# Attention heads in pairs, both token halves transposed in one slot, and another piece left unshifted

## The chip, the cores and the metric

The kernel runs on one core of a Trainium2 chip. The metric is the device time of one execution in microseconds, the median of the runs shown; lower is better.

## What is computed

One layer of a hybrid decoder trunk, 256 tokens by 2048 channels, all float32:

```
h    = rms_norm(x, gain)
proj = einsum('bsd,de->bse', h, w_in)      # 2048 x 8192: h_conv b c z_conv q k v z_attn, 1024 columns each
conv = b * causal_conv_width3(c * h_conv);  y_conv = rms_norm(conv) * silu(z_conv)
q, k = rms_norm per head (8 heads x 128)
s    = q k^T * 128**-0.5, masked to k_pos <= q_pos      # SEQ is one block, so plain causal attention
attn = softmax(s) v;                        y_attn = rms_norm(attn) * silu(z_attn)
out  = x + concat(y_conv, y_attn) @ w_out   # 2048 x 2048
```

## The kernel before

**Products.** Every large product is made from parts: an operand is split into a high half (`wh`, `xs[..., 0]`, `yh`, type fp32r) and the rest (`wl`, `xs[..., 1]`, `yl`), and three products replace one (`by_parts`, L111 to L113; for the channel-major units two instructions, L489 with 512 moving columns for both halves of x and L490 with 256). An fp32r product is one record in the trace. A few small products have plain f32 operands instead, here called *whole*: the q and k transposes (L229, four of 128x128 a call), the first quarter of a head's scores (L258), the transposes of the probabilities (L289, three a head) and the second half of the values' product (L305). A whole product that is no transpose is two records.

**Pieces.** The weights come in 160 pieces of 512 KB, each read by a DMA into `raw` (three buffers), split by ScalarE into `wh` (L481) and by VectorE into `wl` (L482; five buffers each), and used by TensorE. 48 pieces are of kind A (q, k, v for two column halves c: q0 k0 v0 q1 k1 v1, eight pieces each, accumulated token-major in `acc`), then 80 of kind B (20 units of four pieces: the gate `a` of attention, units 0 to 3, then h, c, b, z), then 32 of kind Y (the output product; the last four pieces accumulate in `aux`). They are named A0 to A47, B0 to B79, Y0 to Y31 below; the loop index is j, so B0 is j = 48.

**Order.** The order on each engine is the order of the program text. In iteration j the loop issues the load of piece j+6, the split of piece j+3 and the matmuls of piece j, and then runs what `at(slot, f, ...)` has put under slot j. So all small work stands behind the matmuls of its piece on TensorE, and behind the split of piece j+3 on ScalarE and VectorE. `finish_a` places the work of attention, by the index e of the unit's last piece: for q and k the squares (e+1), norm (e+4, e+5; for q0 later, since it waits for the norm of x), transposes of token half t at e+6+t and their evacuation a slot later (`then`); for v the four heads of the half, head i from slot b = e+2+2i: scores, mask, exponent, normalize, p_transposes, p_transposed, attend, attended at b to b+7. So slots b+4 and b+6 of one head are also slots of the next ones.

**Island.** A run of TensorE instructions between the matmuls of two pieces that holds whole products is called an island here.

**PSUM.** `aux` has four buffers of one bank, used in turn by scores, transposes and values' products; `acc` has two of two banks.

**The shift.** `wh` lies 16 elements further into its buffer in every piece of kind B (`shift`, L465), except in the one piece named by `UNSHIFTED`, a pair (unit, first k-tile):

```
SHIFT, UNSHIFTED = 16, (3, KT // 2)
shift = SHIFT if kind == "B" and (n, k) != UNSHIFTED else 0
```

(3, 8) is B14. Pieces of kind A and Y are not shifted.

Of the kernel before, what the change touches and what calls it, by code (L numbers as in the profile page):

```python
# [17 lines left out]
P = 128  # L18
SEQ = 256
NT = SEQ // P  # L20
DM = 2048
KT = DM // P
DG = 1024
CW = 512
HD = 128
NH = DG // HD
HPC = CW // HD
# [16 lines left out]
SINGLE = 4  # L44
NWARM = 10

SHIFT, UNSHIFTED = 16, (3, KT // 2)


@with_exitstack  # L50
def hybrid_layer(ctx: ExitStack, tc: tile.TileContext, xT, x, w_a, w_b, w_out, par, out):
    nc = tc.nc
# [11 lines left out]
    def aux():  # L64
        return ps.tile([P, CW], F32, name="aux", bufs=4)
# [12 lines left out]
    a = aux()  # L78
    for i in range(NWARM):
        nc.tensor.matmul(a.rearrange("p (a b) -> p a b", b=P), warm, warm[:, None, :].to_broadcast([P, CW // P, P]),  # L80
                         start=i == 0, stop=i == NWARM - 1)
# [18 lines left out]
    def at(slot, f, *args):  # L100
        todo.setdefault(slot, []).append((f, args))
# [6 lines left out]
    def by_parts(acc, stationary, moving, first, last):  # L108

        (sh, sl), (mh, ml) = stationary, moving  # L110
        nc.tensor.matmul(acc, sh, mh, start=first, stop=False)  # L111
        nc.tensor.matmul(acc, sh, ml, start=False, stop=False)  # L112
        nc.tensor.matmul(acc, sl, mh, start=False, stop=last)  # L113
# [83 lines left out]
    qk_0, v_sb, sq, ssq_h, r_h, qn = {}, {}, {}, {}, {}, {}  # L197
# [34 lines left out]
    def k_parts(c):  # L232
        return (y[:, c * HPC:(c + 1) * HPC] for y in (yh, yl))

    def q1_parts(c):
        n = HPC * P // SEQ
        return (y[:, KT // 2 + c * n:KT // 2 + (c + 1) * n].rearrange("p a (b t) -> p (a b) t", t=P) for y in (yh, yl))
# [14 lines left out]

    sc, mx, pr, pT, den = {}, {}, {}, {}, {}

    def scores(h):
        c, i = divmod(h, HPC)
        a = sc[h] = aux()
        nc.tensor.matmul(a[:, :P], qk_0["q", c][:, i], qk_0["k", c][:, i], start=True, stop=True)  # L258
        by_parts(a[:, P:3 * P], [q[:, i] for q in q1_parts(c)], [k[:, i] for k in k_parts(c)], True, True)

    parts = ((0, slice(0, P)), (1, slice(P, 3 * P)))

# [35 lines left out]

    def attend(h):
        c, i = divmod(h, HPC)  # L300
        a = sc[h] = aux()
        vh, vl, v1 = (v[:, i * HD:(i + 1) * HD] for v in v_sb[c])
        hi, lo, p1 = pT[h]
        by_parts(a[:, :SEQ], (vh, vl), (hi, lo), True, False)
        nc.tensor.matmul(a[:, P:SEQ], v1, p1, start=False, stop=True)  # L305

    def attended(h):
        nc.scalar.activation(oT[:, h], sc[h][:, :SEQ], AF.Copy)
# [85 lines left out]
    def finish_a(name, c, acc, e):  # L394
        key, col = (name, c), G_Q if name == "q" else G_K
        late = X_RMS if (name, c) == A_ORDER[0] else 0
        for t in range(NT):
            if name == "v":
                at(e + 1, v_done, c, t, acc[:, t])
            else:  # L400
                at(e + 1, head_squares, key, t, acc[:, t])
                at(max(e + 4 + t, late + 2 ), head_norm, key, t, acc[:, t])
                at(max(e + 6, late + 4) + t, then, max(e + 7, late + 5) + t, head_transposes, head_transposed, key, t, col)
        if name != "v":
            at(e + 2, head_sums, key)
            at(max(e + 2, late + 1), head_rms, key)
            return
        for i in range(HPC):
            h, b = c * HPC + i, e + 2 + 2 * i
            for d, f in enumerate((scores, mask, exponent, normalize, p_transposes, p_transposed, attend, attended)):  # L410
                at(b + d, f, h)

    def finish_b(name, g, acc, e):
        if name == "a":
            at(e + 1, z_done, g, acc)
            at(e + 2, z_silu, g)
            at(A_DONE + 2 * g, lambda: z_gate(g, oT[:, g * GPT:(g + 1) * GPT], KT // 2, G_A))
        elif name == "h":
            at(e + 1, h_done, g, acc)
            at(e + 2, h_scaled, g)  # L420
        elif name == "c":
            at(e + 1, c_done, g, acc)
            at(e + 2, conv, g)
        elif name == "b":
            at(e + 1, b_done, g, acc)
            at(e + 2, lambda: add_squares("c", yc[g]))
        else:
            at(e + 1, z_done, g, acc)
            at(e + 2, z_silu, g)
            at(e + 3, lambda: z_gate(g, yc[g], 0, G_C))  # L430
# [89 lines left out]
    e = ends["B", len(B_ORDER) - 2]  # L520
# [9 lines left out]
    for j, (kind, n, _, k, last, pk, _) in enumerate(pieces):  # L530
# [10 lines left out]
        elif kind == "A":  # L541
            for i in range(pk):
                if j < SINGLE:

                    for n, (s, m) in enumerate(((0, 0), (0, 1), (1, 0))):
                        for t in range(NT):
                            nc.tensor.matmul(acc[:, t], xs[:, k + i, s, t * P:(t + 1) * P], w[m][:, i],
                                             start=k + i == 0 and n == 0, stop=False)
# [5 lines left out]
            if last:  # L554
                finish_a(*A_ORDER[n], acc, j)
# [65 lines left out]
```

## Time and profile before

| | |
|---|---|
| median of 3 runs | 466.1 us (466.03 to 466.13) |
| the profiled execution | 466.41 us, its span 464.6 us, so 1.8 us around it |
| TensorE busy | 458.4 us, 99% of the span |
| VectorE, ScalarE busy | 304.3 us (66%), 241.4 us (52%) |
| weight loads on TensorE (PEld) | 392.0 us (84%) |
| HBM read | 88.11 MB, 194 GB/s over the span |

How to read it: PE is TensorE's matmuls, PEld its weight loads, which overlap them; DVE is VectorE, ACT ScalarE, SP SyncE, which issues the loads. The ends of matmuls are modelled, so they overlap in the rows and busy time says little: the distance from one *start* to the next is what a matmul takes of TensorE's time. A row of a timeline gives start, duration, engine, line, what is written and read, and the count of equal instructions merged.

### The profile page before, as it was taken

How to read it: one execution, taken by the hardware profiler on the slowest of the kernel's cores; microseconds unless marked ns; L12 is line 12 of the kernel's file. 1: busy time of each engine (PE TensorE's matmuls, PEld its weight loads, DVE VectorE, ACT ScalarE, POOL GpSimd, SP SyncE). 2: the span in 40 equal slices, each digit the busy share in tenths (PEclk: the TensorE clock that was granted, in tenths of full speed). 3: DMA queues.
4: the chain of work that ended last, by engine and by line, in shares of the span. 5: the costliest groups of instructions: out<-in, count | busy, mean ns of one | idle time of the engine just before them, and what ended most of it. 6: DMA issues, size and time to landing. Idle time of an engine off the chain costs nothing.

```text
span 464.6 us, 6426 instructions
## 1 busy us (share of the span) xinstructions
PE 458.4 (99%) x2418; PEld 392.0 (84%) x2418; DVE 304.3 (66%) x441; ACT 241.4 (52%) x336; POOL 17.3 (4%) x23
## 2 busy tenths in 40 slices
PE   8999999999999999999999999999999999999996
PEld 5888788888888898888888888888888888888885
DVE  4996866657485657678767676666667775555541
ACT  5965646564535677655645554454545453433320
POOL 1000100002020000000000000000000110001000
PEclk9999999999999999999999999999999999999999
DMA  8977764746565645556666556656666668776731
GB/s 278 299 212 230 231 206 137 223 136 181 141 209 170 200 141 157 172 186 189 213 198 190 192 183 196 204 188 195 193 196 190 190 217 271 231 235 209 247 121 47
DMA packets 27151, 90.63 MB, mean 195 GB/s; under 512 B 3184, under 2 KB 3696, under 8 KB 27120
## 3 DMA queue, kind: packets, MB, share of 16 engines
q1 hardware_dynamic: 26496, 88.51, 60.9%
q0 software_dynamic: 480, 1.57, 1.0%
q8 instruction: 19, 0.31, 0.3%
q10 hardware_dynamic: 144, 0.13, 0.1%
q14 instruction: 12, 0.10, 0.1%
HBM read 88.11 MB, written 2.10 MB: 194 GB/s over the span
## 4 chain that ended last, share of the span: by engine, by line
PE 88%; DMA 4%; DVE 3%; ACT 2%; issue 1%; POOL 0%; SPq 0%; ACTq 0%; DVEq 0%
PE acc L489 31%; PE acc L490 16%; PE acc L111 12%; PE acc L113 12%; PE acc L112 12%; DMA raw<-in_w_a_dram 4%; ACT wh L481 1%; PE aux L111 1%; PE aux L112 1%; PE aux L113 1%; DVE wl L482 1%; PE aux L229 1%; PE aux L289 1%; ACT xs L174 0%; DVE sums_x L130 0%
## 5 line engine op out<-in xcount | busy, mean ns | idle before, releaser
L482 DVE TENSOR_TENSOR wl<-raw,wh 128x1024 fp32r<-128x1024 f32 x156 | 190.5, 1224 | 97.7 <-ACT wh L481 96.8
L481 ACT ACTIVATE wh<-raw 128x1024 fp32r<-128x1024 f32 x156 | 165.0, 1059 | 112.2 <-PE acc L113 53.0
L489 PE MATMUL acc<-xs,wh 128*128 128x512 f32 x640 | 218.6, 390 | 0.0
L490 PE MATMUL acc<-xs,wl 128*128 128x256 f32 x640 | 176.8, 276 | 0.0
L489 PEld LDWEIGHTS acc<-xs,wh 128*128 128x128 f32 x640 | 120.2, 188 | 24.9
L490 PEld LDWEIGHTS acc<-xs,wl 128*128 128x128 f32 x640 | 120.2, 188 | 0.0
L111 PE MATMUL acc<-wh,xs 128*128 128x512 f32 x176 | 69.6, 395 | 0.3 <-DVE t2k L223 0.3
L113 PE MATMUL acc<-wh,xs 128*128 128x512 f32 x176 | 68.6, 390 | 0.0
L112 PE MATMUL acc<-wl,xs 128*128 128x512 f32 x176 | 68.6, 390 | 0.0
L112 PE MATMUL acc<-wl,yh 128*128 128x512 f32 x112 | 43.6, 389 | 0.0
L111 PE MATMUL acc<-wh,yh 128*128 128x512 f32 x112 | 43.6, 389 | 0.0
L113 PE MATMUL acc<-wh,yl 128*128 128x512 f32 x112 | 43.6, 389 | 0.0
L111 PEld LDWEIGHTS acc<-wh,xs 128*128 128x128 f32 x176 | 33.1, 188 | 7.0 <-issue 0.7
L113 PEld LDWEIGHTS acc<-wh,xs 128*128 128x128 f32 x176 | 33.0, 188 | 7.0
L112 PEld LDWEIGHTS acc<-wl,xs 128*128 128x128 f32 x176 | 33.1, 188 | 6.3
L344 ACT ACTIVATE t2k<-acc 128x512 f32<-128x512 f32 x20 | 11.9, 596 | 27.8 <-PE acc L490 27.8
L345 DVE TENSOR_TENSOR t2k<-acc,t2k 128x512 f32<-128x512 f32 x20 | 13.8, 691 | 17.5 <-ACT t2k L344 17.5
L113 PEld LDWEIGHTS acc<-wh,yl 128*128 128x128 f32 x112 | 21.0, 188 | 4.4
L111 PEld LDWEIGHTS acc<-wh,yh 128*128 128x128 f32 x112 | 21.0, 188 | 4.3
L112 PEld LDWEIGHTS acc<-wl,yh 128*128 128x128 f32 x112 | 21.0, 188 | 4.3
L314 ACT ACTIVATE yh<-t2k,prm 128x256 fp32r<-128x256 f32 x16 | 7.3, 502 | 16.8 <-DVE t2k L380 16.8
L116 POOL TENSOR_TENSOR r<-ms,neg_half 128x8 f32<-128x8 f32 x4 | 8.2, 2062 | 79.8 <-DVE ms L216 79.8
(122 smaller groups left out, 313.3 us busy)
## 6 DMA issues: line engine op xcount, KB each, us to landing
raw<-in_w_b_dram SPq DMA_DIRECT2D x80, 512.0 KB, 4.6
raw<-in_w_a_dram SPq DMA_DIRECT2D x44, 512.0 KB, 4.1
raw<-in_w_out_dram SPq DMA_DIRECT2D x32, 512.0 KB, 4.1
raw<-in_w_a_dram SPq DMA_DIRECT2D x8, 256.0 KB, 5.9
t2k<-in_x_dram SPq DMA_DIRECT2D x8, 256.0 KB, 5.2
t2k<-in_xT_dram SPq DMA_DIRECT2D x7, 257.0 KB, 5.5
out_dram<-t2k POOLq DMA_DIRECT2D x6, 256.0 KB, 3.9
out_dram<-t2k SPq DMA_DIRECT2D x1, 256.0 KB, 2.7
```

The lines of the kernel that those rows point to most:

```text
L111: nc.tensor.matmul(acc, sh, mh, start=first, stop=False)
L112: nc.tensor.matmul(acc, sh, ml, start=False, stop=False)
L113: nc.tensor.matmul(acc, sl, mh, start=False, stop=last)
L116: nc.gpsimd.tensor_tensor(dst, ms, neg_half[:, :ms.shape[-1]], op=OP.pow)
L229: nc.tensor.transpose(a[:, i * P:(i + 1) * P], qn[key, t][:, i], ident)
L314: nc.scalar.activation(yh[:, kt + i], src, AF.Copy, scale=g)
L344: nc.scalar.activation(d, acc[:, :, SEQ:], AF.Copy)
L345: nc.vector.tensor_add(d, acc[:, :, :SEQ], d)
L481: nc.scalar.activation(wh, raw, AF.Copy)
L482: nc.vector.tensor_tensor(wl, raw, wh.bitcast(F32), op=OP.subtract)
L489: nc.tensor.matmul(acc[:, b], wh, xs[:, k].rearrange("p s t -> p (s t)"), start=first, stop=False)
L490: nc.tensor.matmul(acc[:, b, :SEQ], wl, xs[:, k, 0], start=False, stop=last)
```

## The change

Heads are handled in pairs (i = 0 and 2 instead of 0 to 3). In `scores` the two whole products of the pair come first, then the parts of both; in `attend` the parts of both, then the two whole products. Each other step runs for both heads in the slot of the first. Both token halves of a q or k are transposed in one slot (and evacuated in the next): the slot that was the second half's. The unshifted piece is (3, 0), B12, instead of B14. No instruction is added or removed.

```diff
-SHIFT, UNSHIFTED = 16, (3, KT // 2)
+SHIFT, UNSHIFTED = 16, (3, 0)
...
     def scores(h):
         c, i = divmod(h, HPC)
-        a = sc[h] = aux()
-        nc.tensor.matmul(a[:, :P], qk_0["q", c][:, i], qk_0["k", c][:, i], start=True, stop=True)
-        by_parts(a[:, P:3 * P], [q[:, i] for q in q1_parts(c)], [k[:, i] for k in k_parts(c)], True, True)
+        for d in range(2):
+            a = sc[h + d] = aux()
+            nc.tensor.matmul(a[:, :P], qk_0["q", c][:, i + d], qk_0["k", c][:, i + d], start=True, stop=True)
+        for d in range(2):
+            by_parts(sc[h + d][:, P:3 * P], [q[:, i + d] for q in q1_parts(c)], [k[:, i + d] for k in k_parts(c)], True,
+                     True)
...
     def attend(h):
         c, i = divmod(h, HPC)
-        a = sc[h] = aux()
-        vh, vl, v1 = (v[:, i * HD:(i + 1) * HD] for v in v_sb[c])
-        hi, lo, p1 = pT[h]
-        by_parts(a[:, :SEQ], (vh, vl), (hi, lo), True, False)
-        nc.tensor.matmul(a[:, P:SEQ], v1, p1, start=False, stop=True)
+        for whole in (False, True):
+            for d in range(2):
+                vh, vl, v1 = (v[:, (i + d) * HD:(i + d + 1) * HD] for v in v_sb[c])
+                hi, lo, p1 = pT[h + d]
+                if not whole:
+                    sc[h + d] = aux()
+                    by_parts(sc[h + d][:, :SEQ], (vh, vl), (hi, lo), True, False)
+                else:
+                    nc.tensor.matmul(sc[h + d][:, P:SEQ], v1, p1, start=False, stop=True)
...
-                at(max(e + 6, late + 4) + t, then, max(e + 7, late + 5) + t, head_transposes, head_transposed, key, t, col)
+                at(max(e + 7, late + 5), then, max(e + 8, late + 6), head_transposes, head_transposed, key, t, col)
...
-        for i in range(HPC):
+        for i in range(0, HPC, 2):
             h, b = c * HPC + i, e + 2 + 2 * i
             for d, f in enumerate((scores, mask, exponent, normalize, p_transposes, p_transposed, attend, attended)):
                 at(b + d, f, h)
+                if f not in (scores, attend):
+                    at(b + d, f, h + 1)
```

TensorE's order at the first scores of the first column half, behind piece A25. Names: `qk_...` are the f32 copies of q and k, `yh` and `yl` here hold the parts of k and of the second half of q, `acc<-wh,xs` is the next piece. Before, one head:

```order
L113 MATMUL acc<-wh,xs 128x512
L258 MATMUL aux<-qk_729,qk_617 128x128
L111 MATMUL aux<-yh 128x256
L112 MATMUL aux<-yl,yh 128x256
L113 MATMUL aux<-yh,yl 128x256
L111 MATMUL acc<-wh,xs 128x512
```

Now, the same place:

```order
L113 MATMUL acc<-wh,xs 128x512
L260 MATMUL aux<-qk_754,qk_635 128x128 x2
L111 MATMUL aux<-yh 128x256
L112 MATMUL aux<-yl,yh 128x256
L113 MATMUL aux<-yh,yl 128x256
L111 MATMUL aux<-yh 128x256
L112 MATMUL aux<-yl,yh 128x256
L113 MATMUL aux<-yh,yl 128x256
L111 MATMUL acc<-wh,xs 128x512
```

The second head's four products have moved here from behind A27, where no island is left. The transposes move in the same way: `L229 ... x4` behind A16 and A17 before, one `L229 ... x8` behind A17 now, and so on for k0, q1 and k1.

TensorE's order at the last island, where attention ends. Before, behind piece B13, with the unshifted B14 after it:

```order
L490 MATMUL acc<-xs,wl 128x256
L111 MATMUL aux<-pTh,vh 128x256
L112 MATMUL aux<-pTl,vh 128x256
L113 MATMUL aux<-pTh,vl 128x256
L305 MATMUL aux<-pT_1842,v_1437 128x128
L489 MATMUL acc<-xs,wh 128x512
L490 MATMUL acc<-xs,wl 128x256
```

Now, behind B11, with the unshifted B12 after it:

```order
L500 MATMUL acc<-xs,wl 128x256
L111 MATMUL aux<-pTh,vh 128x256
L112 MATMUL aux<-pTl,vh 128x256
L113 MATMUL aux<-pTh,vl 128x256
L111 MATMUL aux<-pTh,vh 128x256
L112 MATMUL aux<-pTl,vh 128x256
L113 MATMUL aux<-pTh,vl 128x256
L313 MATMUL aux<-pT_1781,v_1437 128x128
L313 MATMUL aux<-pT_1787,v_1437 128x128
L499 MATMUL acc<-xs,wh 128x512
L500 MATMUL acc<-xs,wl 128x256
```

The last island stands two pieces earlier and ends in two whole products. The islands stood before behind A16, A17, A21, A22, A25, A27, A29, A31, A33, A35, A37, A38, A45, A46 and B1, B3, B5, B7, B9, B11, B13: 14 and 7. Now they stand behind A17, A22, A25, A29, A31, A33, A35, A38, A46 and B1, B5, B7, B9, B11: 9 and 5.

## Rows read from the trace of the kernel before

**Rows 1.** The page: busy time, share of the span and instructions of each engine; then the stretch that holds all islands: its length, busy time of PE, PEld, DVE, ACT and POOL with counts, the granted TensorE clock, the DMA engines' share and GB/s.

```profile
PE 458.4 (99%) x2418; PEld 392.0 (84%) x2418; DVE 304.3 (66%) x441; ACT 241.4 (52%) x336; POOL 17.3 (4%) x23
50.00:200.00 150.00, 149.70 (x794) 128.15 (x793) 98.20 (x168) 87.83 (x143) 6.60 (x3) 1.00 0.58 177
```

**Rows 2.** The only wait of TensorE's matmuls after the first ten microseconds: line, what it waited for, us in total, times, longest.

```profile
PE acc L111 <- DVE t2k L223: 0.3, 1, 0.3
```

**Rows 3.** Timeline of TensorE, the second matmul of A16, the first of A41, A42, B0, B16, B17 and Y0.

```profile
51.60 0.40 PE L112 MATMUL acc<-wl,xs 128*128 128x512 f32 x1
...
128.59 0.39 PE L111 MATMUL acc<-wh,xs 128*128 128x512 f32 x1
...
131.31 0.39 PE L111 MATMUL acc<-wh,xs 128*128 128x512 f32 x1
...
148.58 0.40 PE L489 MATMUL acc<-xs,wh 128*128 128x512 f32 x1
...
198.28 0.39 PE L489 MATMUL acc<-xs,wh 128*128 128x512 f32 x1
...
201.00 0.39 PE L489 MATMUL acc<-xs,wh 128*128 128x512 f32 x1
...
372.59 0.40 PE L111 MATMUL acc<-wh,yh 128*128 128x512 f32 x1
```

**Rows 4.** TensorE's groups by line and shape from 51.29 to 148.58 us: count, then busy time, mean ns of one, idle before.

```profile
L111 PE MATMUL acc<-wh,xs 128*128 128x512 f32 x128 | 50.9, 398 | 0.3 <-DVE t2k L223 0.3
L229 PE MATMUL aux<-ident,t2k 128*128 128x128 f32 x32 | 4.8, 272 | 0.0
L289 PE MATMUL aux<-ident,p 128*128 128x128 f32 x12 | 2.0, 272 | 0.0
L305 PE MATMUL aux<-pT,v 128*128 128x128 f32 x8 | 1.5, 273 | 0.0
L258 PE MATMUL aux<-qk,qk 128*128 128x128 f32 x8 | 1.5, 274 | 0.0
```

**Rows 5.** The same from 148.58 to 372.59 us.

```profile
L489 PE MATMUL acc<-xs,wh 128*128 128x512 f32 x640 | 218.6, 390 | 0.0
L289 PE MATMUL aux<-ident,p 128*128 128x128 f32 x12 | 2.0, 273 | 0.0
L258 PE MATMUL aux<-qk,qk 128*128 128x128 f32 x8 | 1.5, 273 | 0.0
L305 PE MATMUL aux<-pT,v 128*128 128x128 f32 x8 | 1.5, 272 | 0.0
```

**Rows 6.** Timeline of TensorE at an island: behind A31, the second half of the first head's values and the transposes of the second head's probabilities; then one of transposes, behind A16, and seven matmuls on.

```profile
99.58 0.39 PE L305 MATMUL aux<-pT,v 128*128 128x128 f32 x2
99.80 0.49 PE L289 MATMUL aux<-ident,p 128*128 128x128 f32 x3
100.13 0.28 PE L258 MATMUL aux<-qk,qk 128*128 128x128 f32 x1
...
53.89 0.40 PE L113 MATMUL acc<-wh,xs 128*128 128x512 f32 x1
54.12 0.60 PE L229 MATMUL aux<-ident,t2k 128*128 128x128 f32 x4
54.48 0.48 PE L111 MATMUL acc<-wh,xs 128*128 128x512 f32 x1
...
55.95 0.39 PE L111 MATMUL acc<-wh,xs 128*128 128x512 f32 x1
```

**Rows 7.** Timeline of TensorE behind B9: the island's last transposes, the second L489 of B10, and the last L489 of B11.

```profile
179.90 0.49 PE L289 MATMUL aux<-ident,p 128*128 128x128 f32 x3
...
180.58 0.40 PE L489 MATMUL acc<-xs,wh 128*128 128x512 f32 x1
...
185.48 0.39 PE L489 MATMUL acc<-xs,wh 128*128 128x512 f32 x1
```

**Rows 8.** The same behind B11: the island's last transposes, the second and third L489 of B12.

```profile
186.40 0.49 PE L289 MATMUL aux<-ident,p 128*128 128x128 f32 x3
...
187.08 0.39 PE L489 MATMUL acc<-xs,wh 128*128 128x512 f32 x1
...
187.42 0.39 PE L489 MATMUL acc<-xs,wh 128*128 128x512 f32 x1
```

**Rows 9.** The same behind B13: the last whole product, the second L489 of the unshifted B14, and the first two L489 of B15.

```profile
192.52 0.38 PE L305 MATMUL aux<-pT,v 128*128 128x128 f32 x2
...
193.09 0.40 PE L489 MATMUL acc<-xs,wh 128*128 128x512 f32 x1
...
195.56 0.39 PE L489 MATMUL acc<-xs,wh 128*128 128x512 f32 x1
...
195.90 0.39 PE L489 MATMUL acc<-xs,wh 128*128 128x512 f32 x1
```

**Rows 10.** Groups of VectorE and ScalarE by line and shape (the longer of the two halves of mask and of exponent, the lower part of the transposed probabilities), and what the splits on ScalarE waited for.

```profile
L269 DVE CUSTOM_DVE_ANT_0 s<-aux,msk 128x256 f32<-128x256 f32 x8 | 3.4, 420 | 0.0
L276 ACT ACTIVATE p<-s,mx 128x256 f32<-128x256 f32 x8 | 4.0, 499 | 0.0
L296 DVE TENSOR_TENSOR pTl<-aux,pTh 128x256 fp32r<-128x256 f32 x8 | 3.4, 424 | 7.3 <-ACT pTh L295 7.3
ACT wh L481 <- PE acc L489: 41.2, 31, 1.7
```

## The prediction, made before the changed kernel had run

> **What bounds the kernel now.** I read the page first: TensorE is busy for 99% of the span, VectorE and ScalarE for 66% and 52% [rows 1]. Then the waits: after the first ten microseconds TensorE waits once, 0.3 us before A16, for the norm that frees q0's accumulator [rows 2]. That norm stands ahead of everything the change touches, so this wait stays. From there on TensorE alone sets the end, and only the distance between starts of its matmuls can move. The change removes no instruction, so the question is how much of these distances is more than the plain rate.
>
> The plain rates come from undisturbed pieces. A41 takes 131.31 - 128.59 = 2.72 us for 12 products, 0.2267 each; B16 takes 201.00 - 198.28 = 2.72 us for eight pairs of L489 and L490, 0.340 a pair [rows 3], of which 0.227 for 512 columns leaves 0.113 for 256. Whole records follow each other at 0.11: five from 99.58 to 100.13 [rows 6].
>
> With these I count two stretches. From 51.60 to 148.58 (A16 to A47) there are 383 products of pieces (3 x 128 less the one that waited), 32 + 12 + 8 + 8 whole records [rows 3, 4], and 26 of 256 columns (four heads by three of scores and three of values, two of a row sum). 383 x 0.2267 + 60 x 0.11 + 26 x 0.113 = 86.8 + 6.6 + 2.9 = 96.4 us, against 96.98 measured: 0.61 us too much. From 148.58 to 372.59 (all of B): 640 pairs, 12 + 8 + 8 whole records [rows 3, 5] and again 26: 217.6 + 3.1 + 2.9 = 223.6, against 224.01: 0.38 us too much. Together about 1.0 us is all that islands cost beyond their instructions, and so a ceiling on what the change can win.
>
> **Where this 1.0 us lies.** In A, at the way back from whole products to the pieces. From 53.89 to 55.95 there are seven products of 512 columns and four whole: 1.59 + 0.44 = 2.03, measured 2.06 [rows 6], with ten-nanosecond rows. So 0.03 to 0.05 an island; by the sum, 0.61 / 14 = 0.044.
>
> In B something else is seen. Behind B9 the pairs do not go back to 0.340: from 180.58 to 185.48 fourteen take 4.90, 0.350 each, up to the next island [rows 7]. Behind B11, after the same kind of transposes, they are at 0.340 from the second pair on [rows 8]. Behind B13 the unshifted B14 takes 193.09 to 195.56 for seven pairs, 0.353 each, and B15, shifted again, is at 0.340 at once [rows 9]. So TensorE has two rhythms in B, entered at an island that ends in whole products: a fast one that holds for the 65 pieces after B14 (195.56 to 372.59 is 177.03, 65 x 2.72 and two products of 0.113 [rows 3, 9]), and a slow one that holds too while pieces are shifted. The unshifted piece is slow itself but hands over to the fast one. The slow stretch costs 15 x 0.010 = 0.15, B14 7 x 0.013 = 0.09; the rest, 0.38 - 0.24 = 0.14, is 0.02 for each of seven islands.
>
> **The change part by part.**
>
> *Fewer islands in A:* 14 become 9. If an island's price is one of the way back, five are saved: 5 x 0.044 = 0.22. If it goes with the number of whole records, which stays at 60, nothing is saved. Rows 6 show the loss around the return to the piece, so I take 0.22; bounds 0 and 0.22.
>
> *Fewer islands in B:* 7 become 5, at 0.02: 0.04 saved; bounds 0 and 0.04.
>
> *Where B returns from whole products.* Before: behind B9 (slow for two pieces), B11 (fast), B13 (unshifted). Now: behind B7, B9 and B11, the last one before the unshifted B12. B8 and B10 are shifted, and each can be slow for two pieces (0.15) or not; of the two shifted returns on record one was slow. So 0, 0.15 or 0.30, against 0.15 before; I take 0.15, no difference.
>
> *The unshifted piece:* B12 instead of B14, both directly behind the last whole product: 0.09 before and after, if the hand-over at B13 goes as at B15. What it costs if not is the first rival.
>
> *Pairs on VectorE and ScalarE.* Each slot now holds two heads: another mask, lower part and exponent. With the longer half taken twice these are 2 x 0.420 + 0.424 on VectorE and 2 x 0.499 on ScalarE, 2.3 us if they stood one behind the other [rows 10], and as much less two slots on. The cover: splits run three pieces, 8.2 us, ahead of their use, and ScalarE's splits waited 31 times on TensorE to give a buffer back [rows 10], so they are as far ahead as the ring allows. Without that cover each microsecond late would be one on the path. Behind a waiting mask on VectorE stand the next split and its piece, three pieces away. The `aux` buffers: a slot takes four at most (two transposed, two scores), freed one slot later, and the next user comes two slots later. Nothing here is on the path: 0. No DMA is moved and SP's order is unchanged.
>
> *Both halves of q and k in one slot:* the later half keeps its slot, and evacuations wait for both halves as before: 0 beyond the islands.
>
> **Sum.** 0.22 + 0.04 = 0.26 saved, within 0.1 (both returns slow) and 0.41 (both fast). Against the profiled execution 466.41 - 0.26 = 466.15; the median lies 0.3 below it, so 466.1 - 0.26 = 465.84. I forecast 465.8, 0.06% less. A measurement of this kernel tells 0.2%, 0.93 us, from no change.
>
> **Rivals.**
>
> 1. *The slow rhythm stays after attention.* If B13 takes over from the unshifted B12 in the slow rhythm, nothing resets it until the row sums behind B77: 65 pieces x 8 pairs x 0.010 = 5.2 us, 466.1 - 0.26 + 5.2 = 471.0, slower by 1.1%. For it: one hand-over alone is on record, and B14 runs in a slow pattern that could end elsewhere; a stretch of two slow shifted pieces did not heal by itself [rows 7]. Against it: B12 follows whole products as B14 did, and runs the same eight pairs. It decides from fifteen slow pieces on (15 x 8 x 0.010 = 1.2, less the saving, is over 0.93). Chance 0.12.
>
> 2. *Islands cost by their records, not by their number.* Then the change only moves 1.0 us about: 466.1, between 465.95 and 466.25 by the returns behind B7 and B9. For it: a run of eight transposes doubles what is between two pieces, and six parts follow two whole products in a row. Against it: rows 6. Chance 0.20.
>
> 3. *The islands become free.* If the longer runs let TensorE return in step, up to 0.99 would go: 465.1. Against it: every one of the 14 in A shows a loss on the average. Chance 0.03, about the only way to more than 0.2%.
>
> 4. *A clump makes a piece late.* Were two heads' work and a split to use up the 8.2 us, TensorE would wait and each wait would add to the end: with 1 us, 466.8. The added 2.3 us are under a third of the cover. Chance 0.02.
>
> 5. *The clock falls at the longer transposes.* The granted clock is 1.00, the 2.4 GHz level, over all islands [rows 1], in which TensorE ran transposes four at a time amid products. Eight in a row are 0.88 us. If it fell to 1.2 GHz for one piece, that piece would take 5.4 instead of 2.7: 466.1 + 2.7 = 468.5 after the saving. Chance 0.02. The Trainium skill, "TensorE: Matmul & The Clock Gate", "Part 4: PE-mode transpose", says that transposes do not count as activity towards the full clock as other products do. By that rule longer runs of them speak against this change; in this trace islands of up to four left the clock at 1.00.
>
> **How the numbers follow.** The forecast has 0.61, rival 2 0.20, rival 1 0.12, rival 3 0.03, rivals 4 and 5 0.02 each. The predicted time is the forecast's, with its own range 465.6 to 466.1. The range 465.3 to 466.6 adds rival 2 and a margin for a third slow stretch and the spread of the runs, and leaves out rivals 1, 4 and 5 and most of 3: some 0.18. Faster by over 0.2%: rival 3, 0.03. Slower: rivals 1, 4 and 5, 0.16. The rest, 0.81, is the same.
>
> **What the changed profile would show.** Nine islands from A17 to A46 and five from B1 to B11; the stretch from A16's second product to B0 shorter by 0.2; no new wait of TensorE; B13 to B76 at 2.72 a piece. B8 to B11 at 2.72 or 2.80 tell the two returns. Pairs of 0.350 behind B13 would show rival 1, the same sum of excess with fewer islands rival 2. I am wrong if a wait of TensorE on VectorE or ScalarE is new, or if B at large leaves 2.72.

## The result, and the profile after

The changed kernel takes 472.74 us (median of 4 runs, 471.92 to 473.71) beside 466.06 for the kernel before (4 runs, 465.37 to 466.13): a ratio of 1.0149, 95% interval 1.0133 to 1.0166, so slower by 6.7 us. The forecast was 465.8, a change too small to be told; the time lies 1.7 us beyond the first rival's 471.0. The profiled execution took 473.44 us, its span is 471.6, 7.0 longer than before.

First the page's busy times, then windows of it (the granted clock is the column before the last two), then TensorE's one wait after the first ten microseconds, as in [rows 1, 2]:

```profile
PE 465.2 (99%) x2418; PEld 395.3 (84%) x2418; DVE 303.7 (64%) x441; ACT 241.0 (51%) x336; POOL 18.2 (4%) x23
```

```profile
50.00:200.00 150.00, 149.29 (x789) 127.74 (x788) 97.07 (x167) 86.93 (x142) 7.53 (x3) 1.00 0.57 177
200.00:370.00 170.00, 170.00 (x964) 147.85 (x963) 112.87 (x137) 85.37 (x107) 0.00 (x0) 1.00 0.59 187
```

```profile
PE acc L111 <- DVE t2k L223: 0.7, 1, 0.7
```

TensorE is still busy 99% of the span, still waits once, and the clock stays at 1.00. Nothing waits for the pairs, so rivals 4 and 5 are out at once. The 7 us are in the distances between starts. Timeline of TensorE, the rows that answer [rows 3]: second product of A16, the firsts of B0, B13, B14, B15 and Y0.

```profile
51.53 0.40 PE L112 MATMUL acc<-wl,xs 128*128 128x512 f32 x1
...
148.34 0.40 PE L499 MATMUL acc<-xs,wh 128*128 128x512 f32 x1
...
190.22 0.40 PE L499 MATMUL acc<-xs,wh 128*128 128x512 f32 x1
...
193.04 0.40 PE L499 MATMUL acc<-xs,wh 128*128 128x512 f32 x1
...
195.87 0.40 PE L499 MATMUL acc<-xs,wh 128*128 128x512 f32 x1
...
379.62 0.40 PE L111 MATMUL acc<-wh,yh 128*128 128x512 f32 x1
```

A16 to A47: 148.34 - 51.53 = 96.81, 0.17 *less* than before. B: 379.62 - 148.34 = 231.28, 7.27 *more*. Together 7.1, the change of the span. B14 takes 195.87 - 193.04 = 2.83 where a piece took 2.72, 0.353 a pair. The group of L499 grew by much the same, from 218.6 us in [rows 5] (its records overlap, so this is a sign and not a sum):

```profile
L499 PE MATMUL acc<-xs,wh 128*128 128x512 f32 x640 | 225.7, 395 | 0.0
```

And it ends where the first rival said, at the row sums behind B77 (the first two rows are B77's last two pairs):

```profile
373.24 0.40 PE L499 MATMUL acc<-xs,wh 128*128 128x512 f32 x1
...
373.59 0.40 PE L499 MATMUL acc<-xs,wh 128*128 128x512 f32 x1
...
373.95 0.28 PE L141 MATMUL aux<-row_h,ones 128*128 128x256 f32 x1
374.06 0.28 PE L142 MATMUL aux<-row_l,ones 128*128 128x256 f32 x1
374.18 0.39 PE L499 MATMUL acc<-xs,wh 128*128 128x512 f32 x1
...
374.52 0.39 PE L499 MATMUL acc<-xs,wh 128*128 128x512 f32 x1
```

A pair takes 0.35 ahead of the two products, and 0.34 from the first pair behind them. The lines and shapes are the same on both sides.

### The profile page after: what moved, and what is told of

Its sections match the earlier page's. It is cut to its first block, busy times and chain, and to the rows that moved or that the text cites. A ratio compares the mean times of both kernels' runs of the same rounds, so it can differ in the third digit from the quotient of the medians.

```text
span 471.6 us, 6428 instructions
## 1 busy us (share of the span) xinstructions
PE 465.2 (99%) x2418; PEld 395.3 (84%) x2418; DVE 303.7 (64%) x441; ACT 241.0 (51%) x336; POOL 18.2 (4%) x23
## 4 chain that ended last, share of the span: by engine, by line
PE 88%; DMA 4%; DVE 3%; ACT 2%; issue 1%; SPq 0%; POOL 0%; ACTq 0%; DVEq 0%
PE acc L499 32%; PE acc L500 16%; PE acc L111 12%; PE acc L112 12%; PE acc L113 12%; DMA raw<-in_w_a_dram 4%; ACT wh L491 1%; PE aux L111 1%; PE aux L112 1%; PE aux L113 1%; DVE wl L492 1%; PE aux L229 1%; PE aux L293 1%; DVE xs L175 0%; PE aux L260 0%
## 5 line engine op out<-in xcount | busy, mean ns | idle before, releaser
L499 PE MATMUL acc<-xs,wh 128*128 128x512 f32 x640 | 225.7, 395 | 0.0
L500 PE MATMUL acc<-xs,wl 128*128 128x256 f32 x640 | 179.4, 280 | 0.0
L499 PEld LDWEIGHTS acc<-xs,wh 128*128 128x128 f32 x640 | 120.0, 188 | 28.6
L116 POOL TENSOR_TENSOR r<-ms,neg_half 128x8 f32<-128x8 f32 x4 | 9.2, 2294 | 78.9 <-DVE ms L216 78.9
```

The lines of the kernel that those rows point to most:

```text
L116: nc.gpsimd.tensor_tensor(dst, ms, neg_half[:, :ms.shape[-1]], op=OP.pow)
L499: nc.tensor.matmul(acc[:, b], wh, xs[:, k].rearrange("p s t -> p (s t)"), start=first, stop=False)
L500: nc.tensor.matmul(acc[:, b, :SEQ], wl, xs[:, k, 0], start=False, stop=last)
```

## Experiments

The experiments' profiles are read by the length of pieces, the distance from the first L489 (L499 and the like in the other kernels) of one piece to that of the next. The theories are those on record: the hand-over or rhythm theory (TensorE keeps a fast or a slow rhythm, taken up at a break), and against it that the pairs themselves, the place of the unshifted piece, or something beside TensorE makes the difference. Each ratio is to runs of the kernel before from the same session, whose medians were 465.62 to 465.80. The medians are of 2 to 11 runs; the kernels fall into two groups that do not overlap, with no run above 468.13 in the faster one and none below 469.45 in the slower.

| kernel | us, median | ratio to before, 95% | pieces from B15 |
|---|---|---|---|
| pairs_b14 | 472.12 | 1.0137 (1.0121 to 1.0154) | 2.83 |
| singles_b12 | 473.28 | 1.0155 (1.0131 to 1.0179) | 2.83 |
| pairs_none | 465.98 | 1.0004 (0.9992 to 1.0016) | 2.72 |
| singles_none | 472.97 | 1.0155 (1.0133 to 1.0178) | 2.83 |
| pairs_pill13 | 466.24 | 1.0007 (0.9996 to 1.0018) | 2.72 |
| pairs_b14_16 | 466.01 | 1.0006 (0.9992 to 1.0019) | 2.72 from B17 |
| singles_b14_15 | 472.86 | 1.0150 (1.0128 to 1.0171) | 2.83 from B16 |
| pairs_shift32 | 473.17 | 1.0156 (1.0134 to 1.0179) | 2.81 to 2.82 |
| pairs_shift8 | 472.77 | 1.0158 (1.0140 to 1.0177) | 2.81 |
| pairs_both16 | 472.81 | 1.0159 (1.0141 to 1.0178) | 2.83 |
| pairs_wl16 | 470.02 | 1.0099 (1.0081 to 1.0118) | 2.77 |
| mixed | 465.58 | 1.0001 (0.9984 to 1.0017) | 2.72 |

### The two halves of the change apart

The unshifted piece back at B14, in the changed kernel (*pairs_b14*):

```diff
-SHIFT, UNSHIFTED = 16, (3, 0)
+SHIFT, UNSHIFTED = 16, (3, 8)
```

> The changed kernel with the unshifted piece back at B14, so the pairs alone. Hand-over theory (the 7 us come from the shifted B13 taking over a slow rhythm from the unshifted B12): B12 and B13 may be slow, B14 hands over to the fast rhythm as before, B15 to B76 at 2.72 us a piece, 465.6 to 466.2. Pair theory (the island of pairs, which ends in two whole products, leaves a slow rhythm that no unshifted piece ends): B15 to B76 stay at 2.80 to 2.83, 471 to 474.

The move alone, in the kernel before (*singles_b12*):

```diff
-SHIFT, UNSHIFTED = 16, (3, KT // 2)
+SHIFT, UNSHIFTED = 16, (3, 0)
```

> The kernel before with the unshifted piece at B12, so the move alone; its last island stands behind B13, and B14 is shifted. Hand-over theory: the return to the shifted B14 directly behind whole products takes the slow or the fast rhythm and keeps it to B77: 471 to 473 or 466, more likely slow (0.6). Pair theory: without pairs nothing is slow for long, 466.0 to 466.2.

Neither half alone is harmless: 472.12 and 473.28. The second is what the hand-over theory held likelier. The first missed the hand-over theory's 465.6 to 466.2. It has the time that the pair theory gave, but not its reason: B12 and B13 are fast there, so the pairs' last island leaves no slow rhythm, and it is the unshifted B14 that spoils a fast one. In singles_b12 the unshifted B12 hands a slow rhythm to B13, as in the changed kernel, though its heads are single: the last pair of B12 and the first of B13.

```profile
189.29 0.39 PE L489 MATMUL acc<-xs,wh 128*128 128x512 f32 x1
...
189.64 0.40 PE L489 MATMUL acc<-xs,wh 128*128 128x512 f32 x1
...
189.99 0.40 PE L489 MATMUL acc<-xs,wh 128*128 128x512 f32 x1
```

The exact starts of B13's pairs are 350 and 357 ns apart in turn. One island follows, behind B13, and B14 on are slow too. The timeline of pairs_b14, from B13's last L499 into B14, and from B14's last two into B15:

```profile
191.63 0.39 PE L499 MATMUL acc<-xs,wh 128*128 128x512 f32 x1
...
191.97 0.40 PE L499 MATMUL acc<-xs,wh 128*128 128x512 f32 x1
...
192.32 0.40 PE L499 MATMUL acc<-xs,wh 128*128 128x512 f32 x1
...
194.09 0.40 PE L499 MATMUL acc<-xs,wh 128*128 128x512 f32 x1
...
194.44 0.40 PE L499 MATMUL acc<-xs,wh 128*128 128x512 f32 x1
...
194.81 0.40 PE L499 MATMUL acc<-xs,wh 128*128 128x512 f32 x1
...
195.16 0.40 PE L499 MATMUL acc<-xs,wh 128*128 128x512 f32 x1
```

A pair of 0.34, then at the first unshifted product 0.35 and more, in a turn of three lengths (350, 361 and 349 ns by the exact starts); the last of its eight pairs is a long one (194.81 - 194.44 = 0.37), and B15, shifted, runs at 0.35. In the kernel before the unshifted piece ended differently; this is the stretch between two rows of [rows 9]:

```profile
194.85 0.40 PE L489 MATMUL acc<-xs,wh 128*128 128x512 f32 x1
...
195.21 0.40 PE L489 MATMUL acc<-xs,wh 128*128 128x512 f32 x1
```

0.36, then 0.35 up to 195.56: the long one was the last but one, and B15 was fast. This suggests that the unshifted piece is no cure, but a turn of three that happened to stop at the right place; the runs that count the turns, below, test it.

### Without any unshifted piece

In the changed kernel (*pairs_none*); in the kernel before (*singles_none*) the same line goes from `(3, KT // 2)` to `(99, 0)`, which names no piece.

```diff
-SHIFT, UNSHIFTED = 16, (3, 0)
+SHIFT, UNSHIFTED = 16, (99, 0)
```

> The changed kernel with every piece of kind B shifted. Hand-over theory: the return to the shifted B12 decides, fast (465.7) or slow to B77 (471 at 0.350 a pair, 472.5 at 0.353), even chances. Pair theory: slow, 471 to 474.

> The kernel before with every piece of kind B shifted. Hand-over theory: the return to the shifted B14 behind whole products is slow and stays so to B77, 471 to 473 (that the unshifted piece does something). If the unshifted piece does nothing, or the pairs are the cause: 466.1.

With pairs and every piece shifted the time is 465.98, the kernel before's; with single heads and every piece shifted 472.97. So the changed kernel needs no unshifted piece, while the kernel before does. The return is fast in the former, behind its last island, and slow in the latter. First pairs_none, B12; then singles_none, the first product of B14 and of B15 and B16, which are 2.82 apart by these rows (2.83 on the average from there):

```profile
186.37 0.60 PE L313 MATMUL aux<-pT,v 128*128 128x128 f32 x4
186.73 0.48 PE L499 MATMUL acc<-xs,wh 128*128 128x512 f32 x1
...
187.16 0.39 PE L499 MATMUL acc<-xs,wh 128*128 128x512 f32 x1
...
187.50 0.39 PE L499 MATMUL acc<-xs,wh 128*128 128x512 f32 x1
```

```profile
192.62 0.48 PE L489 MATMUL acc<-xs,wh 128*128 128x512 f32 x1
...
195.52 0.40 PE L489 MATMUL acc<-xs,wh 128*128 128x512 f32 x1
...
198.34 0.40 PE L489 MATMUL acc<-xs,wh 128*128 128x512 f32 x1
```

Leaving B12 unshifted turns the first of these into the changed kernel, which is the whole 6.7 us. The pair theory is out. The unshifted piece served single heads behind a return that was slow (B14); moved along with the island it stands behind one that is fast, and spoils it.

### Ending the rhythm, and counting its turns

Two narrow products behind B13 of the changed kernel (*pairs_pill13*), written after the slot's other work:

```diff
         for f, args in todo.pop(j, ()):
             f(*args)
+        if j == ends["A", len(A_ORDER) - 1] + 14:
+            a = aux()
+            for first in (True, False):
+                nc.tensor.matmul(a[:, :SEQ], ones, xs[:, 0, 0], start=first, stop=not first)
```

> The changed kernel with two more products of 256 columns (ones by a slice of x, into a PSUM bank that nobody reads) behind B13, as the row sums behind B77 are. Rhythm theory (TensorE keeps a slow rhythm that it took up behind the unshifted B12, and two narrow products end it): B14 to B76 at 2.72 a piece, 473.4 - 63 x 0.107 + 0.23 = 466.9, at or a little below the kernel before. Outside theory (something that the pairs changed beside TensorE, such as writes of VectorE or ScalarE, slows its reads): no effect, 473 to 474.

```profile
192.72 0.40 PE L499 MATMUL acc<-xs,wh 128*128 128x512 f32 x1
...
193.08 0.39 PE L596 MATMUL aux<-xs,ones 128*128 128x256 f32 x2
193.31 0.39 PE L499 MATMUL acc<-xs,wh 128*128 128x512 f32 x1
...
193.65 0.39 PE L499 MATMUL acc<-xs,wh 128*128 128x512 f32 x1
...
364.67 0.39 PE L499 MATMUL acc<-xs,wh 128*128 128x512 f32 x1
```

Slow up to the two products, 0.34 a pair behind them, and 63 pieces of 2.72 to the first of B77 (364.67 - 193.31 = 171.36): 466.24 instead of 472.74. VectorE, ScalarE and the loads have the same work in the same order in both, so the outside theory is out: the 7 us are a state of TensorE's own stream. The two products also take an `aux` buffer, but the pairs are at 0.34 long before the next user of `aux`, the row sums behind B77.

Then the turns were counted: three unshifted pieces with pairs (B14 to B16), where one gave 472; two with single heads (B14 and B15), where one gives the kernel before. The edit is the same in both; `UNSHIFTED` becomes `((3, 8), (3, 12), (4, 0))` and `((3, 8), (3, 12))`.

```diff
-        shift = SHIFT if kind == "B" and (n, k) != UNSHIFTED else 0
+        shift = SHIFT if kind == "B" and (n, k) not in UNSHIFTED else 0
```

> The changed kernel with three unshifted pieces, B14, B15 and B16, where B14 alone gave 472. In the unshifted B14 of that run the pairs came as 350, 361, 349 ns in turn, and B15 took over behind a 361; in the kernel before B15 took over behind a 349, fast. Rhythm theory: the turn goes on through 24 pairs, the last is a 349, B17 takes over fast, 465.6 to 466.6. Place theory (what counts is the buffer or the k-tile that the unshifted piece has, not the turn): three unshifted pieces are no better than one, 472 to 473.

> The kernel before with two unshifted pieces, B14 and B15, where B14 alone is the kernel before. Rhythm theory: with 16 pairs in turns of three the last is a 361, B16 takes over slow, 472 to 473.5. Place theory: B14 has set the fast rhythm and B15 only adds its 0.1, 466.2; or B15 is a bad place, slow.

466.01 and 472.86, as the rhythm theory had it and the place theory had not. The three pieces' end, in pairs_b14_16, and the first pair of B17:

```profile
199.19 0.40 PE L499 MATMUL acc<-xs,wh 128*128 128x512 f32 x1
...
199.55 0.40 PE L499 MATMUL acc<-xs,wh 128*128 128x512 f32 x1
...
199.90 0.39 PE L499 MATMUL acc<-xs,wh 128*128 128x512 f32 x1
...
200.24 0.39 PE L499 MATMUL acc<-xs,wh 128*128 128x512 f32 x1
```

0.36, 0.35, then 0.34: the long pair is the last but one again, and two more slow pieces make the kernel 6 us faster than with B14 alone. In singles_b14_15 the last pair of B15 is the long one, and B16 is slow:

```profile
197.60 0.40 PE L489 MATMUL acc<-xs,wh 128*128 128x512 f32 x1
...
197.97 0.40 PE L489 MATMUL acc<-xs,wh 128*128 128x512 f32 x1
...
198.32 0.40 PE L489 MATMUL acc<-xs,wh 128*128 128x512 f32 x1
```

So of the ends in these four kernels, two behind a long pair were slow and two a pair later were fast. An end at the third place of the turn was not tried.

### Other offsets

```diff
-                  for m, o in (("wh", shift), ("wl", 0)))
+                  for m, o in (("wh", shift), ("wl", shift)))
```

This is pairs_both16; pairs_wl16 has `(("wh", 0), ("wl", shift))` there, pairs_shift32 and pairs_shift8 have `SHIFT` 32 and 8. None has an unshifted piece.

> The changed kernel with all pieces of kind B shifted, by 32 elements instead of 16. With 16 it is at 466.0 with slow stretches behind B1 (three pieces, 0.08 each) and B9 (two, 0.09). Rhythm theory has no number for another shift: if the offset between the two streams of reads sets which rhythms can hold, pieces change their length, 2.72 everywhere (465.6) or slow ones everywhere (up to 474); if the shift only has to be other than zero, the same as with 16, 466.0.

> The changed kernel with all B pieces shifted by 8 elements. 16 has a fast rhythm, 0 and 32 have shown none. If only the one distance serves: 2.80 to 2.83 a piece, 472 to 474. If every offset between 0 and 32 serves, 465.6 to 466.5.

> The changed kernel with wh and wl both shifted by 16 elements in all B pieces. With wh alone shifted it runs at 466.0, fast at 2.72 from B12 on. If the fast rhythm needs wh and wl at different offsets, it is gone here as with no shift: 2.80 or more a piece, 472 to 474. If it needs wh or wl at an offset to x, it stays, 465.6 to 466.2.

> The changed kernel with wl alone shifted by 16 elements in all B pieces, wh at its buffer's start. If the fast rhythm needs wh and wl at different offsets, by any sign: 2.72 from B12 or so on, 465.6 to 466.5. If it needs wh at 16 elements to x, it is gone: 472 to 474.

None keeps the fast rhythm. With 32, B78, right behind the row sums, is slow at once, 376.90 - 374.09 = 2.81:

```profile
374.09 0.39 PE L499 MATMUL acc<-xs,wh 128*128 128x512 f32 x1
...
376.90 0.39 PE L499 MATMUL acc<-xs,wh 128*128 128x512 f32 x1
```

So of the offsets tried only `wh` at 16 and `wl` at its buffer's start holds pairs at 0.340. `wl` alone at 16 has a rhythm of its own, 0.347, and its 470.02 is neither of the times expected for it; its B15 and B16 start 2.78 apart by these rows, 2.77 on the average:

```profile
195.12 0.39 PE L499 MATMUL acc<-xs,wh 128*128 128x512 f32 x1
...
197.90 0.39 PE L499 MATMUL acc<-xs,wh 128*128 128x512 f32 x1
```

The other three lie between 0.351 and 0.353. No kernel had both at their buffers' start in all pieces; single unshifted pieces took 0.347 or 0.353 a pair.

### Pairs only where they paid

Pairs for heads 0 to 3 beside A, single heads beside B, B14 unshifted (*mixed*; c is the column half):

```diff
-        for i in range(0, HPC, 2):
+        m = 1 if c else 2
+        for i in range(0, HPC, m):
```

with `scores` and `attend` taking m heads.

> Pairs in the first column half (heads 0 to 3, beside the A pieces) and both halves of every q and k transposed in one slot, but single heads in the second column half, whose islands lie between B pieces, and B14 unshifted as in the kernel before. Rhythm theory: A17 to A47 keep the 0.26 us that the pairs saved there, the B pieces are as in the kernel before (B10 and B11 slow, B14 slow, fast from B15), so 0.26 below it, 465.5 to 465.6 beside a median of 465.8, which is inside what can be told. Outside theory: where pairs stand makes no difference, B is slow from B15, 472.

From the second product of A16 to B0 its trace has 96.79 us, against 96.98 before; B takes 224.01, as before. The median is 465.58 against 465.62, ratio 1.0001 (0.9984 to 1.0017): the 0.2 us that the trace shows can't be told by the times, whose runs differ by over 2 us, mostly in the first 50 us (A16 begins at 49.8 to 51.5 in the traces of all kernels, while from Y0 to the end they all take 92.0). It beats the changed kernel by 7 us, and the kernel before by nothing that can be measured.

## Why the prediction was wrong, point by point

- *The bound and the ceiling* held: TensorE's starts alone decide, its one wait stays, and no kernel tried gained anything that can be told.
- *Fewer islands in A*: 0.22 forecast, 0.17 measured (96.98 against 96.81). The same stretch takes 96.77 to 96.83 in all ten kernels with pairs there and 96.97 to 97.00 in the four without, so fewer islands do save, and rival 2 is wrong in A.
- *Pairs on VectorE and ScalarE, buffers, clock*: 0 forecast, no new wait, clock 1.00.
- *Fewer islands in B*: 0.04 forecast, not seen. By exact starts B13 to B77 cost 6.92 of the 7.27 us, B2 to B5 0.31 (below), and the slow pairs of B10 to B12 0.02 more than those of B10, B11 and B14 before; the 0.02 left over is no saving.
- *Where B returns*, forecast 0.15 for two open returns. B8 came back fast, B10 slow for two pieces, as allowed. But a third return was not on the list: behind B1 six parts follow the whole products, and B2 to B5 are slow up to the next island, 0.08 each (two rows of the changed kernel: the first products of B2 and B3, 2.80 apart). The prediction put this return at nothing without a reason; before, with three parts behind the whole products, B2 was fast (2.72).

```profile
154.96 0.39 PE L499 MATMUL acc<-xs,wh 128*128 128x512 f32 x1
...
157.76 0.39 PE L499 MATMUL acc<-xs,wh 128*128 128x512 f32 x1
```

  This alone, 0.31, gives back the 0.2 won in A. In pairs_none, which has no unshifted piece, B takes 372.01 - 147.73 = 224.28 (its first rows of B0 and Y0), 0.27 more than before. So even without the step below the change would have brought nothing.

```profile
147.73 0.40 PE L499 MATMUL acc<-xs,wh 128*128 128x512 f32 x1
...
372.01 0.40 PE L111 MATMUL acc<-wh,yh 128*128 128x512 f32 x1
```

- *The unshifted piece*, "0.09 before and after, if the hand-over at B13 goes as at B15": the step that failed. I read [rows 9] as a piece that hands over to the fast rhythm. It was one stop of a turn, seen once, and in the changed kernel the unshifted B12 does not even run that turn. It settles on pairs of 0.347 and hands a slow rhythm to B13:

```profile
189.52 0.39 PE L499 MATMUL acc<-xs,wh 128*128 128x512 f32 x1
...
189.86 0.39 PE L499 MATMUL acc<-xs,wh 128*128 128x512 f32 x1
```

  Here B12's last two pairs: 0.347 and 0.352 by the exact starts, up to B13 at 190.22; 187.78 to 189.52, five pairs of 0.348 on the average, stand ahead of them. So the condition of that step, the same hand-over at B13 as at B15, did not come about: B13 to B77 cost 6.9 us where the forecast had nothing.
- *The first rival* was the right mechanism with its place and its end. Its price was too low: 65 pieces at 0.350 a pair, 5.2 us. It took the slow rhythm of [rows 7], but there is a second one, 0.353, and B13 took up that one: 65 pieces, B13 to B77, times 8 x 0.0133 = 0.107 are 6.9. (The second is not peculiar to unshifted pieces: B10 of the changed kernel and B14 on in singles_none have it behind an island.) Its chance, 0.12, was too low as well: one hand-over on record, out of a pattern that visibly alternated, was, in hindsight, no ground for seven to one. And [rows 8] showed a shifted B12 that came back fast by itself, if behind another island; a kernel with B12 left shifted, which is pairs_none and costs nothing that can be told, was not weighed.

## What to carry to other kernels

Where an engine's stream has no waits left, look at the distance between starts by piece: a loss of 3% that repeats from piece to piece may be a lasting state, and then what matters is what starts and ends it. A tuned constant that ends such a state, as the unshifted piece did here, belongs to the very sequence ahead of it; when the sequence changes, try the kernel without the constant first. And a single instance of a hand-over is a coin seen once: give the other side its chance.

## What the runs showed of the hardware

Weight loads and matmuls of this stream (512 and 256 moving columns, a new 128-column weight for each) lock into rhythms that depend on where the weights lie in SBUF: 0.340 us a pair with the high part's weights 16 elements into their buffer, 0.347 to 0.353 at the other offsets tried. At that same offset there are slow rhythms too: 0.353, which lasted 65 pieces in the changed kernel, and 0.350, which lasted up to the next island, at most four pieces. Which is taken is set at a break and is repeatable: in the profiles of the kernels with pairs at 16 elements (one of each) B2 to B4 take 2.80 and B6 2.72 each time, and in the kernel before the same island (values, then transposes) leads to slow when entered from fast pieces (B10) and to fast when entered from slow ones (B12). At 16 elements two products of 256 columns ended the slow rhythm each time that it had lasted, at the row sums of all five kernels that were slow up to B77 and in pairs_pill13, but six in a row behind whole products started one (B2).

The Trainium skill, "TensorE: Matmul & The Clock Gate", "Step-by-step: what each phase is for", says that TensorE has two independent read ports, so that loading the next weights takes no read bandwidth from the running matmul. Here the offsets of the weights alone moved a pair from 0.340 to as much as 0.353, so where the weights lie does count for the pace of the products; where the page leads one to expect no difference, the measurement decides. Whether the two reads meet, or what else in the offset counts (VectorE and ScalarE write to the moved place as well), no run here settles; nor was it tried why six narrow products lead to another rhythm than three or two.

Eight transposes in a row left the granted clock at 1.00, the 2.4 GHz level, as four had.
